# Seven gates of the attention branch given out ahead of the recurrences' merge, and that merge's first two outputs together

## The chip, the cores and the metric

One core of one Trainium2 chip runs the program. The metric is the device time of one execution in microseconds (us), the median over runs without a profile. The engines are TensorE (PE; its weight loads are PEld), VectorE (DVE), ScalarE (ACT), GpSimd (POOL) and SyncE (SP), which issues the loads.

## What is computed

Two transformer blocks run one after the other on 512 tokens of width 1024, in fp32. The change touches the second block, which has two layers (0 and 1). Cut to what matters here, a layer is:

```python
h = rmsnorm_2(x, norm_mix[l])
proj = h @ w_in[l]
aq, ak, av, iq, ik, iw, hq, hf, hi, hg, ga, gb = jnp.split(proj, split_points, axis=-1)
y_attn = dsa_attention(aq, ak, av, iq, ik, iw)          # top-k attention, 8 heads
...
o = hgrn2_chunked(q_h, k_in, v_h, log_f)                # gated recurrence, 4 heads
y_hgrn = (rmsnorm_2(o, hgrn_norm[l]) * silu(hg)).reshape(B, T, HGRN_WIDTH)
merged = sigmoid(ga) * (y_attn @ w_proj_attn[l]) + sigmoid(gb) * (y_hgrn @ w_proj_hgrn[l])
x = x + merged @ w_out[l]
h = rmsnorm_2(x, norm_ffn[l])
g, u = jnp.split(h @ w_ffn_in[l], 2, axis=-1)
x = x + (silu(g) * u) @ w_ffn_out[l]
```

A *gate* below is one 128-wide slice of ga or gb: eight gates for each of the two branches. The sigmoid is made from a tanh, and the factor of a half that is left is taken up at the residual sum.

## The kernel before, in words

Activations lie transposed, 128 features by 512 tokens to a tile. Every fp32 product is made from three matmuls: operands are split into a high part (a cast to fp32r) and a low part (what is left), and low x high, high x low and high x high are summed in PSUM.

**Weights** (`weights`, lines 133 to 154). A load of SP's queue brings 512 KB (or 256 KB for the output weights of a branch, which have four slices) into one of three `wraw` buffers. Per *set* of four 128x128 slices ScalarE casts the high part (line 149), and GpSimd or VectorE subtracts to give the low part (line 152). Which of the two is read off a rotation, `self.lows` (GpSimd, GpSimd, VectorE in the mixing stages), with a running count of sets. There are three buffers for the high and three for the low parts. A set feeds 12 matmuls of 128x512. All this is traced with high priority.

**Projections** (`project`, lines 184 to 196, the three matmuls on lines 193 to 195). Eight slices give 24 matmuls (a gate, from the two sets of one load), four slices give 12 (an output of a branch). The sum goes to one of four PSUM banks of the tag `mm`. `project_pair` (lines 198 to 217) makes two outputs at once and leaves the last slice of both to the end, so that the last input tile is wanted late.

**A gate** (`gate`, lines 694 to 698) is projected, evicted to SBUF by VectorE with the norm's factor (line 223) and put through tanh by ScalarE (line 697). Its tile is of the tag `g`, five slots.

**The merge of a branch** (`merge`, lines 700 to 718) makes `ahead` gates, then for each of eight outputs m the gate m + ahead, if there is one left, the projection of the branch, and the product (gate + 1) x projection on VectorE (line 710), with high priority. In the last merge of a layer the product is added to what the other branch left (line 715): on GpSimd for outputs 0 to 3, on VectorE for outputs 4 to 7, and from output 4 on all weight sets subtract on GpSimd. The sum is then split for the next projection: a cast on ScalarE (`mgh`, line 232), a subtraction on VectorE (`mgl`, line 233).

**A layer** (`second_mix`, lines 990 to 1016) traces, in this order: the attention (`dsa`, lane `a`, whose work tiles are of the tag `ua` with seven slots; its last tile is `aon`, line 969, and the next layer's first is `rows`, line 860, with four table products on lines 868 and 869), the four heads of the recurrence (lane `h`, tag `uh`, seven slots; a head's first tile is the `tanh` of its q, line 690, its last the `ry`, line 439), the recurrences' merge (two gates ahead) and the attention's merge (four gates ahead). After that comes the output projection (`residual`, lines 720 to 737), whose first two outputs are a pair.

**What sets the order.** A scheduler turns the traced program into one fixed queue per engine when the program is built: an instruction that was traced earlier has priority, one that is ready may run ahead of one that isn't. On the chip every queue is worked off in that order.

Of the kernel before, what the change touches and what calls it, by code (L numbers as in the profile page):

```python
# [21 lines left out]
KD = 8  # L22
# [48 lines left out]
class Builder:  # L71
# [340 lines left out]
    def recurrence(self, qi, kl, dec, v, AT, gate, gain, scale, name):  # L412
        nc = self.nc
        klT = self.u("rklT", shape=[P, NT, P])
        self.transpose4(kl, klT)
        kv = self.at([P, NT - 1, P])
        for t in range(NT - 1):
            nc.tensor.matmul(kv[:, t, :], klT[:, t, :], v[t], start=True, stop=True)
        S = self.u("rS", shape=[P, NT - 1, P])
        nc.vector.tensor_copy(S[:, 0, :], kv[:, 0, :])  # L420
        for t in range(1, NT - 1):
            nc.vector.scalar_tensor_tensor(S[:, t, :], S[:, t - 1, :], dec[:, t:t + 1], kv[:, t, :],
                                           op0=OP.mult, op1=OP.add)
        o = self.at([P, NT, P])
        for t in range(NT):
            nc.tensor.matmul(o[:, t, :], AT[:, t * P:(t + 1) * P], v[t], start=True, stop=t == 0)
            if t:
                nc.tensor.matmul(o[:, t, :], qi[:, t * P:(t + 1) * P], S[:, t - 1, :], start=False, stop=True)
        sq = self.u("rsq", shape=[P, NT, P])
        nc.scalar.activation(sq, o, AF.Square)  # L430
        ss = self.small("rss", NT)
        nc.vector.reduce_sum(ss, sq, axis=AX.X)
        nc.vector.tensor_scalar(ss, ss, scale / P, EPS, op0=OP.mult, op1=OP.add)
        r = self.rsqrt(ss, NT)
        on = self.u("ron", shape=[P, NT, P])
        nc.vector.tensor_tensor(on, o, r[:, :, None].to_broadcast([P, NT, P]), op=OP.mult)
        ps = self.transpose4(on.rearrange("p n c -> p (n c)"), None)
        y = self.u("ry")
        nc.vector.scalar_tensor_tensor(y, ps.rearrange("p n c -> p (n c)"), gain, gate, op0=OP.mult, op1=OP.mult)
        return self.split(y, name)  # L440

    def gla_head(self, B, q, k, v, gate, gain, name):
        nc = self.nc
        s = 1.0 / 16
# [44 lines left out]
    def hgrn_head(self, F, q, k, v, gate, gain, name):  # L489
# [6 lines left out]
        nc.vector.copy_predicated(AT, self.masks[:, T:2 * T], ps.rearrange("p n c -> p (n c)"))  # L496
        G = self.u("hG")
        for i, h in enumerate(LEVELS + (64,)):
            n = T // (2 * h)
            X = self.u("lvx")  # L500
            if h < 64:
                mk = self.masks[:, 2 * T + i * 256:2 * T + (i + 1) * 256].rearrange("p (n r) -> p n r", n=n)
            Fv, Gv, qv, kv, Xv, Av = [a.rearrange("p (n s r) -> p n s r", n=n, s=2) for a in (F, G, q, k, X, AT)]
            if h == 1:
# [30 lines left out]
        nc.vector.tensor_tensor(F, F, q, op=OP.mult)  # L535
        nc.gpsimd.tensor_tensor(G, G, k, op=OP.mult)
        return self.recurrence(F, G, dec, v, AT, gate, gain, 0.25, name)

# [152 lines left out]
        self.nc.vector.scalar_tensor_tensor(x, t, 1.0, x, op0=OP.add, op1=OP.mult)  # L691
        return x

    def gate(self, src, X):
        g = self.g("gate")
        self.evict(g, self.project(src, X))
        self.nc.scalar.activation(g, g, AF.Tanh, scale=0.5)
        return g

    def merge(self, W, X, WO, y, acc, ahead, last, alloc=None):  # L700
        nc = self.nc
        G = [self.gate(W[m], X) for m in range(ahead)]
        out = []
        for m in range(KD):
            if m + ahead < KD:
                G.append(self.gate(W[m + ahead], X))
            g = G[m] if acc else (alloc or self.t)("acc")
            ps = self.project(WO[m], y)
            with self.tc.high_priority():
                nc.vector.scalar_tensor_tensor(g, G[m], 1.0, ps, op0=OP.add, op1=OP.mult)  # L710
            if acc:
                eng = nc.vector if last and m + ahead >= KD else nc.gpsimd
                if last and m + ahead == KD:
                    self.lows = [nc.gpsimd]
                eng.tensor_tensor(acc[m], acc[m], g, op=OP.add)
                g = acc[m]
            out.append(self.split(g, "mg") if last else g)
        return out
# [271 lines left out]
    def second_mix(self, l, X):  # L990
        nc, A = self.nc, self.A
        W = A["w_in2"][l]
        it = iter(range(W.shape[0]))
        proj = lambda: self.project(W[next(it)], X)

        with self.on("a"):
            yattn = self.dsa(l, X)
        if self.pending:
            self.settle()
        hv = self.hv  # L1000
        yh = []
        for hd in range(4):
            F = self.scaled(proj(), "hf", self.i)
            k = self.i("hk")
            nc.scalar.activation(k, F, AF.Sigmoid, scale=-1.0)
            nc.scalar.activation(F, F, AF.Sigmoid)
            if l:
                nc.gpsimd.tensor_scalar(k, k, self.om[:, hd:hd + 1], None, op0=OP.mult)
                nc.vector.tensor_scalar(F, F, self.om[:, hd:hd + 1], self.lb[:, hd:hd + 1], op0=OP.mult, op1=OP.add)
            q = self.silu2(proj(), "hq")  # L1010
            v = [a[:, hd * P:(hd + 1) * P] for a in hv]
            g = self.silu2(proj(), "hg")
            yh.append(self.hgrn_head(F, q, k, v, g, self.half[:, 4 + l:5 + l], "yh"))

        acc = self.merge(A["w_gate2"][l, 1], X, A["w_po"][l, 1], yh, None, 2, False, self.i)
        return self.merge(A["w_gate2"][l, 0], X, A["w_po"][l, 0], yattn, acc, 4, True)

    def build(self, out):
        nc, A = self.nc, self.A
# [118 lines left out]
```

## Time and profile before

| | |
|---|---|
| median of the runs | 2522.63 us (2522.59 to 2522.65) |
| profiled execution | 2524.49 us |
| its span, first to last instruction | 2522.7 us |
| instructions | 31514 |
| PE, DVE, ACT, POOL busy | 2488.7, 1369.4, 1007.2, 614.2 us |
| granted TensorE clock, mean | 0.997 |

Times in the rows are counted from the start of the span. In layer 0 the attention and the recurrence take about 880 to 1178 us, the two merges 1178 to 1290, the output projection up to 1330; in layer 1 these are about 1700 to 2007, 2007 to 2118, and up to 2158. A row of the timeline has the start, the duration, the engine, the line of the kernel, the operation, what is written from what, the shapes, how many instructions are put together, and in brackets how long the engine was idle before it and what ended that. Matmuls overlap, so that their pace is read off their starts.

### The profile page before, as it was taken

The numbers are of one execution on the slowest core, as the hardware profiler recorded it, in microseconds if no ns is written. First come the engines' busy times: TensorE is split into PE (matmuls) and PEld (weight loads), VectorE is DVE, ScalarE is ACT, GpSimd is POOL, SyncE is SP. The second block draws the span as 40 slices with busy tenths as digits, with TensorE's granted clock in tenths as the row PEclk, the third lists the DMA queues.
The fourth block names the chain that finished last, engine by engine and source line by source line (L and its number), as shares of the span: only waits on it lengthen the run. The fifth ranks groups of instructions, "written<-read, shape, count | busy, mean of one in ns | idle before, by whom it ended". The sixth has DMA issues, their size and how long they took to land.

```text
span 2522.7 us, 31514 instructions
## 1 busy us (share of the span) xinstructions
PE 2488.7 (99%) x11742; PEld 2038.2 (81%) x11742; DVE 1369.4 (54%) x2696; ACT 1007.2 (40%) x1830; POOL 614.2 (24%) x548
## 2 busy tenths in 40 slices
PE   9999999999999999999999999999999999999999
PEld 7887888888888887777888888888777788888887
DVE  4675222477774558986244444334798624444432
ACT  5643333444443345543343333334554334333321
POOL 4004344511111102433361111010253435111100
PEclk9999999999999999999999999999999999999999
DMA  4112232322323322111332232332211133232333
GB/s 140 59 61 84 88 100 92 105 92 100 100 91 99 92 92 76 43 38 53 96 100 96 97 101 90 100 90 95 81 42 38 39 97 104 92 101 92 98 104 90
DMA packets 68298, 217.66 MB, mean 86 GB/s; under 512 B 7840, under 2 KB 8736, under 8 KB 68144
## 3 DMA queue, kind: packets, MB, share of 16 engines
q1 hardware_dynamic: 68144, 215.65, 26.7%
q8 instruction: 92, 1.51, 0.3%
q14 instruction: 62, 0.51, 0.1%
HBM read 213.52 MB, written 2.10 MB: 85 GB/s over the span
## 4 chain that ended last, share of the span: by engine, by line
PE 85%; DVE 7%; issue 3%; POOL 2%; ACT 2%; DMA 0%; SPq 0%; DVEq 0%; POOLq 0%; ACTq 0%
PE mm L195 23%; PE mm L194 23%; PE mm L193 23%; PE mm L168 3%; PE mm L169 3%; PE mm L170 3%; PE at L953 1%; DVE score L915 1%; PE at L965 1%; DVE m L914 1%; POOL wlo L152 1%; POOL hG L516 1%; PE at L260 1%; PE at L961 1%; DVE wlo L152 1%
## 5 line engine op out<-in xcount | busy, mean ns | idle before, releaser
L149 ACT CAST whi<-wraw 128x512 fp32r<-128x512 f32 (+3 forms) x824 | 502.1, 610 | 1120.6 <-PE mm L195 918.5
L194 PE MATMUL mm<-xl,whi 128*128 128x512 f32 x1920 | 758.2, 395 | 0.0
L193 PE MATMUL mm<-xh,wlo 128*128 128x512 f32 x1920 | 757.4, 395 | 0.0
L195 PE MATMUL mm<-xh,whi 128*128 128x512 f32 x1920 | 756.4, 394 | 0.0
L152 DVE TENSOR_TENSOR wlo<-wraw,whi 128x512 fp32r<-128x512 f32 (+2 forms) x597 | 428.3, 718 | 494.8 <-ACT whi L149 491.5
L152 POOL TENSOR_TENSOR wlo<-wraw,whi 128x512 fp32r<-128x512 f32 (+1 forms) x227 | 294.7, 1299 | 784.6 <-ACT whi L149 723.6
L194 PEld LDWEIGHTS mm<-xl,whi 128*128 128x128 f32 x1920 | 361.2, 188 | 73.8 <-issue 1.7
L195 PEld LDWEIGHTS mm<-xh,whi 128*128 128x128 f32 x1920 | 361.2, 188 | 73.7 <-issue 1.7
L193 PEld LDWEIGHTS mm<-xh,wlo 128*128 128x128 f32 x1920 | 361.1, 188 | 71.8 <-issue 0.7
L193 PE MATMUL mm<-acth,wlo 128*128 128x512 f32 x528 | 205.4, 389 | 0.0
L195 PE MATMUL mm<-acth,whi 128*128 128x512 f32 x528 | 205.4, 389 | 0.0
L194 PE MATMUL mm<-actl,whi 128*128 128x512 f32 x528 | 205.4, 389 | 0.0
L763 POOL TENSOR_TENSOR fg<-fg,rstd 128x512 f32<-128x512 f32 x44 | 56.6, 1287 | 425.9 <-ACT fg L762 425.9
L168 PE MATMUL mm<-wlo,xh 128*128 128x512 f32 (+2 forms) x384 | 144.1, 375 | 5.1 <-ACT lbe L813 3.6
L170 PE MATMUL mm<-whi,xh 128*128 128x512 f32 (+2 forms) x384 | 143.4, 374 | 0.0
L169 PE MATMUL mm<-whi,xl 128*128 128x512 f32 (+2 forms) x384 | 142.6, 371 | 0.0
L223 DVE TENSOR_TENSOR gate<-mm,rstd 128x512 f32<-128x512 f32 x56 | 38.7, 691 | 151.3 <-PE mm L195 150.5
L194 PEld LDWEIGHTS mm<-actl,whi 128*128 128x128 f32 x528 | 99.1, 188 | 20.7
L193 PEld LDWEIGHTS mm<-acth,wlo 128*128 128x128 f32 x528 | 99.1, 188 | 20.6
L195 PEld LDWEIGHTS mm<-acth,whi 128*128 128x128 f32 x528 | 99.1, 188 | 20.4
L298 POOL TENSOR_TENSOR acc<-acc,sq 128x512 f32<-128x512 f32 x39 | 57.6, 1478 | 200.5 <-ACT sq L295 199.6
L168 PEld LDWEIGHTS mm<-wlo,xh 128*128 128x128 f32 x384 | 72.8, 190 | 19.3 <-issue 4.5
(362 smaller groups left out, 3236.0 us busy)
## 6 DMA issues: line engine op xcount, KB each, us to landing
wraw<-in_w_ffn_in SPq DMA_DIRECT2D x88, 512.0 KB, 3.3
wraw<-in_w_gate SPq DMA_DIRECT2D x56, 512.0 KB, 3.3
wraw<-in_w_in SPq DMA_DIRECT2D x52, 512.0 KB, 3.2
wraw<-in_w_up SPq DMA_DIRECT2D x44, 512.0 KB, 3.2
wraw<-in_w_tok SPq DMA_DIRECT2D x32, 512.0 KB, 3.2
wraw<-in_w_ffn_out SPq DMA_DIRECT2D x32, 512.0 KB, 3.6
wraw<-in_w_down SPq DMA_DIRECT2D x16, 512.0 KB, 3.5
wraw<-in_w_po SPq DMA_DIRECT2D x32, 256.0 KB, 2.6
```

What stands on the lines that cost most here:

```text
L149: nc.scalar.copy(wh, raw[:, k:k + m, :])
L152: eng.tensor_tensor(wl, raw[:, k:k + m, :], wh.bitcast(F32), op=OP.subtract)
L168: nc.tensor.matmul(ps[t][:, 0:w], xh, wl, start=i == 0, stop=False)
L169: nc.tensor.matmul(ps[t][:, 0:w], xl, wh, start=False, stop=False)
L170: nc.tensor.matmul(ps[t][:, 0:w], xh, wh, start=False, stop=i == KD - 1)
L193: nc.tensor.matmul(ps, wl, xh, start=i == 0, stop=False)
L194: nc.tensor.matmul(ps, wh, xl, start=False, stop=False)
L195: nc.tensor.matmul(ps, wh, xh, start=False, stop=i == n - 1)
L223: self.nc.vector.tensor_tensor(out, ps, other, op=OP.mult)
L260: self.nc.tensor.transpose(ps[:, t, :], src[:, t * P:(t + 1) * P], self.ident)
L298: (nc.vector if d % 2 and len(acc) > 1 else nc.gpsimd).tensor_tensor(a, a, sq, op=OP.add)
L763: nc.gpsimd.tensor_tensor(g, g, self.rstd, op=OP.mult)
```

## The change

`merge` takes gates that were made before (`made`) and then makes only the rest; with `pair` its first two outputs are projected together. In each layer of the second block seven gates of the attention branch are traced ahead of the recurrences' merge, into tiles of the attention's tag `ua`; the attention's merge then has one gate left, which goes with output 0. The recurrences' merge is called with `pair`. The rule that gives the sums to VectorE from output 4 on is written with a constant and is the same as before for four gates ahead; it stays at output 4 for seven.

```diff
-    def gate(self, src, X):
-        g = self.g("gate")
+    def gate(self, src, X, alloc=None):
+        g = (alloc or self.g)("gate")
...
-    def merge(self, W, X, WO, y, acc, ahead, last, alloc=None):
-        nc = self.nc
-        G = [self.gate(W[m], X) for m in range(ahead)]
+    def merge(self, W, X, WO, y, acc, ahead, last, alloc=None, made=(), pair=False):
+        nc = self.nc
+        G = list(made) + [self.gate(W[m], X) for m in range(len(made), ahead)]
         out = []
+        pss = {}
         for m in range(KD):
             if m + ahead < KD:
                 G.append(self.gate(W[m + ahead], X))
             g = G[m] if acc else (alloc or self.t)("acc")
-            ps = self.project(WO[m], y)
+            if pair and m == 0:
+                pss.update(enumerate(self.project_pair([WO[0], WO[1]], y)))
+            ps = pss.pop(m) if m in pss else self.project(WO[m], y)
...
-                eng = nc.vector if last and m + ahead >= KD else nc.gpsimd
-                if last and m + ahead == KD:
+                eng = nc.vector if last and m >= KD // 2 else nc.gpsimd
+                if last and m == KD // 2:
                     self.lows = [nc.gpsimd]
...
-        acc = self.merge(A["w_gate2"][l, 1], X, A["w_po"][l, 1], yh, None, 2, False, self.i)
-        return self.merge(A["w_gate2"][l, 0], X, A["w_po"][l, 0], yattn, acc, 4, True)
+        with self.on("a"):
+            made = [self.gate(A["w_gate2"][l, 0, m], X, self.u) for m in range(self.SLOTS["a"])]
+        acc = self.merge(A["w_gate2"][l, 1], X, A["w_po"][l, 1], yh, None, 2, False, self.i, pair=True)
+        return self.merge(A["w_gate2"][l, 0], X, A["w_po"][l, 0], yattn, acc, len(made), True, made=made)
```

## Rows read from the trace of the kernel before

**Rows 1.** The page: busy time by engine; shares of the chain that ended last.

```profile
PE 2488.7 (99%) x11742; PEld 2038.2 (81%) x11742; DVE 1369.4 (54%) x2696; ACT 1007.2 (40%) x1830; POOL 614.2 (24%) x548
...
PE 85%; DVE 7%; issue 3%; POOL 2%; ACT 2%; DMA 0%; SPq 0%; DVEq 0%; POOLq 0%; ACTq 0%
```

**Rows 2.** Windows: length, busy PE PEld DVE ACT POOL, clock, DMA.

```profile
1110.00:1178.00 68.00, 64.26 (x405) 51.37 (x404) 54.82 (x130) 25.12 (x56) 32.49 (x36) 1.00 0.09 26
1178.00:1290.00 112.00, 112.00 (x494) 92.64 (x495) 36.61 (x53) 37.38 (x61) 41.89 (x33) 1.00 0.30 97
1936.00:2007.00 71.00, 67.46 (x400) 53.12 (x399) 50.80 (x123) 24.21 (x54) 32.90 (x36) 0.95 0.08 25
```

**Rows 3.** Timeline of PE, layer 0, fourth head: start, duration, instruction, idle before.

```profile
1156.82 0.39 PE L530 MATMUL at<-lvx 128*120 128x64 f32 x2 [0.85 <-DVE lvx L514]
...
1158.04 0.47 PE L193 MATMUL mm<-xh,wlo 128*128 128x512 f32 x1
```

**Rows 4.** Windows in layer 1, where the granted clock falls.

```profile
1940.00:1945.00 5.00, 3.28 (x23) 2.90 (x22) 4.04 (x8) 0.48 (x1) 4.69 (x6) 0.89 0.31 107
1945.00:1950.00 5.00, 5.00 (x17) 3.56 (x16) 2.02 (x6) 0.53 (x2) 2.46 (x5) 0.50 0.02 3
```

**Rows 5.** Timeline of DVE, layer 0, third and fourth head.

```profile
1100.02 0.69 DVE L223 TENSOR_TENSOR hq<-mm,rstd 128x512 f32<-128x512 f32 x1 [0.19 <-PE mm L195]
...
1126.76 0.69 DVE L223 TENSOR_TENSOR gate<-mm,rstd 128x512 f32<-128x512 f32 x1
...
1145.30 0.75 DVE L439 SCALAR_TENSOR_TENSOR ry<-at,half,hg 128x512 f32<-128x512 f32 x1 [0.26 <-PE at L260]
...
1166.93 0.69 DVE L969 TENSOR_TENSOR aon<-at,aden 128x512 f32<-128x512 f32 x1 [0.74 <-PE at L965]
...
1168.88 0.41 DVE L868 SCALAR_TENSOR_TENSOR tabC<-cos,rows 128x256 f32<-128x256 f32 x1
```

**Rows 6.** Timeline of ACT, the same stretch.

```profile
1145.40 0.63 ACT L690 ACTIVATE tanh<-hq 128x512 f32<-128x512 f32 x1
```

**Rows 7.** Groups of PE, 1110 to 1178: count, busy, mean ns, idle before.

```profile
L194 PE MATMUL mm<-xl,whi 128*128 128x512 f32 x30 | 12.7, 424 | 0.0
```

**Rows 8.** Timeline of SP's queue in the same stretch.

```profile
1149.96 0.33 SPq L861 DMA_DIRECT2D rows<-in_rows  x1
```

**Rows 9.** Timeline of PE, first output of the recurrences' merge, layer 0.

```profile
1177.87 0.50 PE L193 MATMUL mm<-yhh,wlo 128*128 128x512 f32 x1
```

**Rows 10.** Timeline of DVE, attention's merge, layer 0, outputs 3 to 5.

```profile
1275.27 0.69 DVE L710 SCALAR_TENSOR_TENSOR gate<-gate,mm 128x512 f32<-128x512 f32 x1 [2.03 <-PE mm L195]
1279.28 0.69 DVE L233 TENSOR_TENSOR mgl<-acc,mgh 128x512 fp32r<-128x512 f32 x1 [3.33 <-ACT mgh L232]
1279.89 0.68 DVE L710 SCALAR_TENSOR_TENSOR gate<-gate,mm 128x512 f32<-128x512 f32 x1
1280.61 1.08 DVE L715 TENSOR_TENSOR acc<-acc,gate 128x512 f32<-128x512 f32 x1
...
1282.98 0.68 DVE L710 SCALAR_TENSOR_TENSOR gate<-gate,mm 128x512 f32<-128x512 f32 x1
```

**Rows 11.** Timeline of POOL, the same outputs.

```profile
1276.06 1.29 POOL L152 TENSOR_TENSOR wlo<-wraw,whi 128x512 fp32r<-128x512 f32 x1 [1.43 <-issue]
1277.31 1.29 POOL L715 TENSOR_TENSOR acc<-acc,gate 128x512 f32<-128x512 f32 x1
1279.85 1.29 POOL L152 TENSOR_TENSOR wlo<-wraw,whi 128x512 fp32r<-128x512 f32 x1 [1.25 <-ACT whi L149]
```

**Rows 12.** Timeline of ACT, the same outputs.

```profile
1278.63 0.62 ACT L232 CAST mgh<-acc 128x512 fp32r<-128x512 f32 x1 [2.70 <-POOL acc L715]
1279.15 0.62 ACT L149 CAST whi<-wraw 128x512 fp32r<-128x512 f32 x1
```

**Rows 13.** Timeline of PE, first pair of the output projection, layer 0.

```profile
1293.20 0.39 PE L209 MATMUL mm<-mgh,whi 128*128 128x512 f32 x1
1293.67 0.50 PE L207 MATMUL mm<-mgh,wlo 128*128 128x512 f32 x1
```

## The prediction

> **What bounds the kernel now.** I read the page's busy times and its chain first: TensorE is busy for 2488.7 of 2522.7 us and carries 85% of the chain that ended last [rows 1]. Its work stays the same here, so only its waits can move. The windows by stage say where these are. In the stretch from the merge of the recurrences to the end of the attention's merge TensorE is busy for all of 112 us, with 494 matmuls, 0.227 us each; in the two stretches in which the last recurrence head and the last attention block run, it stands idle for 68.00 - 64.26 = 3.7 us (layer 0) and 71.00 - 67.46 = 3.5 us (layer 1) [rows 2]. The timeline of TensorE shows the kind of these waits: at 1156.82 a small matmul of the recurrence waits 0.85 us for VectorE, and the gate's matmul of 1158.04 stands behind it in the queue [rows 3]. The order is fixed when the program is built, and a matmul that could fill the gap sits behind the one that waits. Between 1945 and 1950 the granted clock is 0.50, the lower level of 1.2 GHz, after TensorE was idle for 1.7 of the 5 us ahead of it [rows 4]. At half speed for 5 us, some 2.5 us are lost.
>
> **Part 1: seven gates go ahead.** Per layer 7 x 24 = 168 matmuls, 14 weight sets (cast on ScalarE, subtraction on GpSimd or VectorE), 7 loads of 512 KB on SP's queue, 7 evictions and 7 tanh move ahead of the recurrences' merge: past its 8 gates and 8 outputs, on every queue. Nothing is added. A set feeds 12 matmuls whichever gate it belongs to, so SP's queue and the casts keep their rate, and the move of the loads costs nothing by itself. The gain would be filler for the waits. But filler was not lacking: in before the gates of the recurrences' merge already stand in this place, the first is evicted at 1126.76 [rows 5], and the gap of 1156 had a gate's matmul right behind it [rows 3]. Another gate in that place is the same filler. I take 0; the best case is that all idle time goes, -3.7 and -3.5 us [rows 2], and the half clock with it, -2.5 us [rows 4].
>
> The new tiles are not free as early. The tanh of a head's q waits for its tile: q is evicted at 1100.02, yet its tanh runs at 1145.40, right after the last tile (ry) of the previous head came at 1145.30 [rows 5, 6], although tanh needs nothing else. So tiles of one tag are given out in the program's order. The gates' tiles then come after the attention's last one, aon, at 1166.93 [rows 5]; until then up to four products stay in PSUM's four mm banks, 96 matmuls. Before used some 90 of such filler between 1110 and 1178 (this line's 30 and two more lines of 30 [rows 7]), and a few more of the merge's, so the banks just suffice: 0, and up to +1 us per layer if they don't. Two evictions of 0.69 us leave the stretch before 1166 and fall behind it: 0, bounds -1.4 and +1.4 us per layer on VectorE; TensorE has gates to do meanwhile. The load of the next layer's rope rows, the next tile of this tag, went out at 1149.96 [rows 8]; it now waits behind the gates for a freed tile, in the attention's merge. Its four table products (0.41 us each, the first at 1168.88 [rows 5]) go there too: 0, bounds -1.7 and +1.7 us, once. SP's later loads stand behind that wait; with three load buffers they run ahead of it, so 0.
>
> **Part 2: the first two outputs together.** Before, the last part of output 0 is mixed with a gate's matmuls, and two matmuls at such a change take 0.1 us longer: the one at 1177.87 has 0.50 us [rows 9], where its like have 0.39 [rows 13]. Now ten gates stand ahead of the pair, 240 matmuls, of which some 90 are done when the last head is; the pair starts 150 x 0.227 = 34 us later, the mixing goes, and with it twice 0.1: -0.2 us per layer. The pairing itself then hides nothing.
>
> **Part 3: the attention's merge loses its gates.** This is the term that decides. Before, outputs 0 to 3 each have a gate beside them: 36 matmuls, 8.17 us. The chain from an output's product (line 710) over the sum on GpSimd, the cast and the low half (line 233) takes 1275.27 to 1279.28 plus 0.61 until the next product can start at 1279.89: 4.62 us [rows 10]. It fits into 8.17, not into the 12 x 0.227 = 2.72 us of an output alone. And VectorE takes low half and next product in that order: at 1279.89 the product of output 4, whose matmuls were done about 1278.0, comes right behind the low half of output 3 [rows 10]. After the change outputs 1 to 3 stand as output 4 does now. Each transition is then a loop of queues that each wait for the other:
> - 0 to 1, with GpSimd's weight subtraction ahead of the sum (1276.06, then 1277.31 [rows 11]): 4.62 us.
> - 1 to 2: the rotation (GpSimd, GpSimd, VectorE; the count before output 4 stays as it is) gives this subtraction to VectorE, so the sum starts at once: 0.72 to the sum, 1.32 to the cast, 0.65 to the low half, 0.61 to the next product [rows 10 to 12], 3.30 us.
> - 2 to 3 and 3 to 4: the cast of a weight set stands behind the cast of the output: 0.52, then 0.70 to the subtraction, 1.25 to the sum, 1.32 to the next cast [rows 11, 12], 3.79 us each.
> Sum 15.5 us; before it was 3 x 2.72 + 4.62 = 12.78 of the same work (gates apart). The lag grows by 2.7 us. From output 4 on, the loop runs at 1279.89 to 1282.98 = 3.09 us against 2.72 [rows 10], as before, and there all reserve of weights is used up: the last set of the output projection's pair already comes late, TensorE goes from 1293.20 to 1293.67 where 0.23 is due, a wait of 0.24 us [rows 13]. So what is added shows in full: **+2.7 us per layer**. Bounds: 0, if VectorE takes the next product first and the loop opens; 4 x 4.62 - 12.78 = +5.7, if each transition takes as long as the first.
>
> **Sum.** 2 x (2.7 - 0.2) = +5.0 us. On the profiled execution (2524.49 us, a span of 2522.7 with 1.8 around it) that is 2529.5; the median of the runs without a profile is 1.86 below, so 2522.63 + 5.0 = **2527.6 us**. Measurement tells 0.2% (5.05 us) from no change, so this is just no change, with slower close by.
>
> **Rivals.**
> - *The loop opens.* VectorE takes the next product while the low half waits; TensorE stays full. For it: the gates are out of the way, and GpSimd's load (a sum of 1.29 and two thirds of a subtraction of 1.29 [rows 11], 2.2 us of 2.72) fits. Against: the order at 1279 [rows 10]. It gives 2522.6 - 0.4 = 2522.2.
> - *The waits in the recurrences go*, since evictions and tables leave that stretch, and the clock doesn't fall: half of 7.3 us of idle time and 2.5 us of clock, with the loop open: 2522.2 - 3.7 - 2.5 = 2516. For it: VectorE is busy for 54.8 of 68 us there [rows 2]; against: the order is fixed as before.
> - *GpSimd and VectorE stop each other* (slower). The sum on VectorE at 1280.61 takes 1.08 us while GpSimd subtracts from 1279.85 to 1281.14; the low half with two inputs of the same size takes 0.69 beside an idle GpSimd [rows 10, 11]. In outputs 0 to 3 GpSimd will be busy most of the time, so low halves and subtractions on VectorE get this 0.4 us at least, in each of four transitions: 2 x 4 x 0.4 = 3.2, 2530.8; with a whole GpSimd instruction of 1.29 each, 2538. It decides once GpSimd runs through without a gap. The Trainium skill ("SBUF — State Buffer", section "SBUF: two separate sides") says that whichever of a GpSimd instruction and a VectorE instruction with two SBUF inputs starts first holds the shared port pair and the other is fully blocked; the trace agrees with it at 1280.61, where the sum ends 0.55 us after the subtraction, and the higher end is what that page would make of it.
>
> **How the numbers follow.** The loop as worked out 0.58 (its own range is 2523.5 to 2531.5, and half of it lies beyond 2527.7); the loop open 0.20; fewer waits in the recurrences 0.12; GpSimd and VectorE in each other's way 0.10. Faster by over 0.2%: 0.12, the third case; slower: 0.36, half of the first and two thirds of the fourth; within: 0.52, the rest. The range leaves out the low end of the third and the high end of the fourth: 2516.5 to 2532.5.
>
> **What would show it.** Products of outputs 1 to 4 at line 710 that start right behind a low half of line 233, 3.3 to 4.6 us apart, and waits of TensorE for a subtraction (line 152) in the last outputs and the pair of the output projection, 2 to 3 us per layer: right. Products 2.72 us apart and no wait: the loop is open. Gates' evictions only after aon: the tile order is right. Idle time from the last head's projections to its end well off 3.7 and 3.5 us: part 1 is wrong.

## The result, and the profile after

The changed kernel takes 2536.2 us (median of four runs, 2533.4 to 2536.6) against 2522.6 us of the kernel before on the same chip: a ratio of 1.0051 (95% interval 1.0039 to 1.0063), 13.6 us slower. The forecast was 2527.6 us with a range up to 2532.5: slower had been given the second largest chance (0.36), and the time lies outside the range. The profiled execution took 2536.1 us, with a span of 2534.3.

The page of the kernel after, busy time by engine (before: [rows 1]), and its windows, with the columns of [rows 2]:

```profile
PE 2493.1 (98%) x11742; PEld 2041.0 (81%) x11742; DVE 1375.5 (54%) x2696; ACT 1007.3 (40%) x1830; POOL 614.0 (24%) x548
```

```profile
1110.00:1178.00 68.00, 62.36 (x395) 50.33 (x394) 53.38 (x124) 24.09 (x54) 32.46 (x36) 1.00 0.09 29
...
1280.00:1302.00 22.00, 20.08 (x82) 14.63 (x82) 12.12 (x16) 7.41 (x14) 10.21 (x8) 1.00 0.34 109
1936.00:2007.00 71.00, 66.24 (x389) 53.40 (x389) 50.84 (x115) 23.72 (x53) 30.06 (x35) 0.90 0.09 30
```

The same window behind the attention's merge, in the kernel before:

```profile
1280.00:1302.00 22.00, 21.92 (x97) 17.81 (x97) 14.22 (x16) 9.12 (x16) 11.68 (x10) 1.00 0.35 120
```

The instructions are the same (11742 matmuls). Two kinds of stretch have become worse, in each layer: the last head of the recurrences, with 5.6 us idle in place of 3.7 (layer 0) and 4.8 in place of 3.5 (layer 1), and the end of the attention's merge, where 15 matmuls fewer fit into 22 us.

Busy time alone hides two losses, matmuls at half clock and such as start late without a recorded wait. So the table below uses **lost time**: for each TensorE instruction the time from its start to the start of the next, less the median of this for its kind (line, shape) in the same run, added up over a stretch. It is worked out from the whole trace of each profiled run.

```
                     heads 1-3     last head     both    end of attention's
                     L0     L1     L0     L1     merges  merge, L0   L1    time - before   ratio (95%)
before               11.7   12.4   6.7    11.0   -0.3    1.1   1.1         0
after                11.7   12.5   8.6    14.7   -0.3    4.4   4.2     +13.6   1.0051 (1.0039-1.0063)
e1_four_ahead        11.7   12.5   8.6    14.9   -0.3    1.1   1.1      +5.4   1.0019 (1.0010-1.0028)
e2_gates_between     11.7   12.5   7.7    10.4    0.1    4.1   4.2      +7.6   1.0028 (1.0017-1.0039)
e3_pair_alone        11.6   12.5   8.2    12.0   -0.2    1.1   1.1      +2.4   1.0009 (1.0000-1.0018)
e4_sums_vector       11.7   12.5   9.7    14.7   -0.3    1.6   1.0      +5.6   1.0020 (1.0011-1.0029)
e5_plain_evict       11.8   12.5   9.5    12.8   -0.3    4.4   4.3     +12.2   1.0047 (1.0034-1.0059)
e6_early_tiles       11.7   12.5   7.9    11.4   -0.3    1.1   1.1      +0.6   1.0001 (0.9992-1.0010)
e7_late_tiles        11.7   12.5   8.2    14.7   -0.3    1.4   1.1      +3.9   1.0014 (1.0005-1.0022)
e8_no_pair           11.7   12.5   9.9    12.5   -0.3    4.3   4.1     +10.7   1.0040 (1.0027-1.0052)
e9_no_subtraction    11.7   12.5   8.3    12.8   -0.3    4.4   4.2     +11.7   1.0044 (1.0031-1.0056)
e10_low_vector        8.6    7.1   8.0    12.2   17.5    1.1   1.1     +12.0   1.0049 (1.0035-1.0063)
e11_both              8.8    8.0   9.5    13.9    0.4    1.1   1.1      -4.3   0.9985 (0.9976-0.9994)
e12_heads_only        8.5    7.7   7.7    14.6    3.0    1.1   1.1      -1.9   0.9995 (0.9986-1.0004)
```

Stretches: 990-1110 and 1800-1925; 1110-1180 and 1925-2015; 1180-1280 and 2015-2110 together; 1280-1345 and 2110-2180. Times are differences of medians against the kernel before, run beside each (2521.8 to 2523.2 us). What is left out of the columns differs by up to 2 us from before, mostly ahead of 990, where the code is the same and the granted clock is 0.50 for 6.8 us in some profiles and for 3.4 in others. Each run has its own medians: in e10, e11 and e12 the attention's matmuls of 128x512 (`at<-kT,qT`) have 0.43 us in place of before's 0.48, and with before's medians the four heads' columns of these three rows, added up, are 1.7 to 2.8 us lower (last heads 7.2 and 11.3, 8.6 and 13.0, 7.1 and 14.0); e7's last heads become 7.8 and 14.3.

After against before: 3.4 + 3.1 us at the end of the attention's merge, 1.9 + 3.7 us in the last head, 12.1 in all (added up before rounding); the span grew by 11.6.

**The end of the merge.** Timeline of VectorE in the kernel after, layer 0, outputs 0 to 5 (start, duration, instruction, idle before; line 713 is the product that was 710, 718 the sum that was 715; compare [rows 10]):

```profile
1268.46 0.69 DVE L713 SCALAR_TENSOR_TENSOR gate<-gate,mm 128x512 f32<-128x512 f32 x1 [2.03 <-PE mm L195]
1272.42 0.69 DVE L233 TENSOR_TENSOR mgl<-acc,mgh 128x512 fp32r<-128x512 f32 x1 [3.28 <-ACT mgh L232]
1273.03 0.68 DVE L713 SCALAR_TENSOR_TENSOR gate<-gate,mm 128x512 f32<-128x512 f32 x1
...
1276.15 0.69 DVE L233 TENSOR_TENSOR mgl<-acc,mgh 128x512 fp32r<-128x512 f32 x1
1276.76 0.68 DVE L713 SCALAR_TENSOR_TENSOR gate<-gate,mm 128x512 f32<-128x512 f32 x1
...
1280.18 0.69 DVE L233 TENSOR_TENSOR mgl<-acc,mgh 128x512 fp32r<-128x512 f32 x1 [0.41 <-ACT mgh L232]
1280.79 0.68 DVE L713 SCALAR_TENSOR_TENSOR gate<-gate,mm 128x512 f32<-128x512 f32 x1
1284.03 0.69 DVE L233 TENSOR_TENSOR mgl<-acc,mgh 128x512 fp32r<-128x512 f32 x1 [2.56 <-ACT mgh L232]
1284.64 0.68 DVE L713 SCALAR_TENSOR_TENSOR gate<-gate,mm 128x512 f32<-128x512 f32 x1
```

Each product starts right behind the low half of the output before it: the loop of queues. The transitions, from one product to the next, are 4.57, 3.73, 4.03 and 3.85 us, 16.2 in all. The sum of the second transition, on GpSimd, takes 1.67 us in place of 1.29 (timeline of GpSimd):

```profile
1273.79 1.67 POOL L718 TENSOR_TENSOR acc<-acc,gate 128x512 f32<-128x512 f32 x1 [2.06 <-DVE gate L713]
```

TensorE runs out of weight sets behind it (timeline of PE; [rows 13] has 0.47 us from the first of such a pair to the second, here it is 1.1):

```profile
1285.93 0.50 PE L193 MATMUL mm<-yah,wlo 128*128 128x512 f32 x1 [0.76 <-POOL wlo L152]
...
1298.39 0.50 PE L207 MATMUL mm<-mgh,wlo 128*128 128x512 f32 x1 [0.75 <-POOL wlo L152]
```

**The last head.** A head's result is brought to its norm: VectorE makes an rsqrt in eleven small steps on 128x4 elements (lines 433 and 250 to 254), multiplies (`ron`, line 436), and TensorE transposes `ron` (line 260). VectorE in the kernel after, layer 0 (compare [rows 5]), with GpSimd's and TensorE's rows of the same moment:

```profile
1167.12 0.69 DVE L972 TENSOR_TENSOR aon<-at,aden 128x512 f32<-128x512 f32 x1 [2.06 <-PE at L968]
1167.72 1.28 DVE L223 TENSOR_TENSOR gate<-mm,rstd 128x512 f32<-128x512 f32 x2
...
1174.24 0.16 DVE L252 TENSOR_TENSOR rsq_w<-rss,rsq_y 128x4 f32<-128x4 f32 x1
...
1174.84 1.21 DVE L252 TENSOR_TENSOR rsq_w<-rss,rsq_y 128x4 f32<-128x4 f32 x1
...
1176.55 0.69 DVE L436 TENSOR_TENSOR ron<-at,rsq_y 128x512 f32<-128x512 f32 x1
```

```profile
1174.74 1.29 POOL L152 TENSOR_TENSOR wlo<-wraw,whi 128x512 fp32r<-128x512 f32 x1 [11.75 <-ACT whi L149]
```

```profile
1177.30 0.66 PE L260 MATMUL at<-csts,ron 128*128 128x128 f32 x4 [1.25 <-DVE ron L436]
```

The first gate is evicted right behind `aon`, not 40 us ahead of it as in [rows 5]. And a step of the head's rsqrt on 128x4 elements, 0.16 us as its like at 1174.24, takes 1.21 us while GpSimd subtracts; it ends with that subtraction, `ron` is late by 1.05 us, and TensorE waits 1.25. In layer 1 the step takes 0.98 and the wait 0.73. Before, GpSimd's subtraction came behind the last step, which ended at 1174.94:

```profile
1176.62 1.30 POOL L152 TENSOR_TENSOR wlo<-wraw,whi 128x512 fp32r<-128x512 f32 x1 [11.51 <-ACT whi L149]
```

**Layer 1 and its clock.** A head works through several levels; in each VectorE and GpSimd fill a tile `lvx` and GpSimd carries on a product `hG`, for small matmuls of TensorE (line 530). GpSimd, VectorE and TensorE in the last head's first levels, then two windows of the kernel after:

```profile
1979.52 1.29 POOL L152 TENSOR_TENSOR wlo<-wraw,whi 128x512 fp32r<-128x512 f32 x1 [9.00 <-ACT whi L149]
1980.77 0.92 POOL L507 TENSOR_TENSOR lvx<-lvx,hk 128x256 f32<-128x256 f32 x1
```

```profile
1979.74 1.34 DVE L518 TENSOR_TENSOR hf<-hf 128x256 f32<-128x256 f32 x1
...
1983.86 0.43 DVE L518 TENSOR_TENSOR hf<-hf 128x256 f32<-128x256 f32 x1 [1.89 <-POOL hG L516]
```

```profile
1986.55 0.62 PE L530 MATMUL at<-lvx 128*124 128x64 f32 x4 [1.98 <-POOL lvx L515]
```

```profile
1985.00:1990.00 5.00, 3.45 (x23) 3.42 (x23) 4.79 (x11) 1.40 (x3) 3.91 (x6) 0.80 0.00 0
1990.00:1995.00 5.00, 5.00 (x19) 3.92 (x19) 2.63 (x7) 0.81 (x2) 2.38 (x4) 0.52 0.00 0
```

A weight subtraction now stands in GpSimd's queue right ahead of the head's first level. VectorE's step at 1979.74 takes 1.34 us beside that subtraction, its like at 1983.86 0.43. The level starts at 1980.77, 1.1 us after its input from VectorE was there, and TensorE waits 1.98 us in the levels. In the kernel before the longest wait in this head's levels is 1.06 us:

```profile
1988.83 0.69 PE L530 MATMUL at<-lvx 128*96 128x64 f32 x6 [1.06 <-DVE AT L532]
```

Behind the wait of 1.98 us the granted clock goes to 0.50, the level of 1.2 GHz, from 1988 to 1994.8. Before had one such stretch in this layer ([rows 4], 1944 to 1951); the kernel after has that one (1947 to 1954) and this one. The four timed runs show the same: three at a mean clock of 0.996 with 2536.1 to 2536.6 us, one at 0.998 with 2533.4.

### The profile page after: what moved, and what is told of

Read it like the earlier page. It is cut to its first block, busy times and chain, and to the rows that moved or that the text cites. A ratio compares the mean times of both kernels' runs of the same rounds, so it can differ in the third digit from the quotient of the medians.

```text
span 2534.3 us, 31505 instructions
## 1 busy us (share of the span) xinstructions
PE 2493.1 (98%) x11742; PEld 2041.0 (81%) x11742; DVE 1375.5 (54%) x2696; ACT 1007.3 (40%) x1830; POOL 614.0 (24%) x548
```

## The experiments

Three theories: **A**, the merge's loop (some 6.5 us); **B**, the gates' late tiles (free only behind `aon`), which change the order of the work in the last head; **C**, GpSimd's subtraction beside the rsqrt. Rivals are that one of them is all of it, or that the move of the gates ahead is the cause, whatever their tiles.

### Taking the loop away, or doing it alone

e1: four gates ahead in place of seven.

```diff
-made = [... for m in range(self.SLOTS["a"])]
+made = [... for m in range(4)]
```

> The changed kernel with four gates of the attention ahead in place of seven; the other four again stand beside outputs 0 to 3 of the attention's merge. Split theory (merge loop about 6.5 us of the 13.6, the rest in the recurrences' end and in the half clock): the loop is gone and the rest stays, 2536.2 - 6.5 = about 2529.7 us, with transitions between the products of outputs 0 to 3 back at about 8 us and no TensorE waits over 0.2 us behind 1280. Rival 'all of it is the merge loop' (the waits in the recurrences would have moved, not grown): 2522.6 us. Rival 'all of it is the recurrences' end': about 2536 us.

Measured 2528.3 us, +5.4. The end of the merge loses 1.1 us again, with 21.92 of 22 us busy; the last head is as in the kernel after.

```profile
1280.00:1302.00 22.00, 21.92 (x98) 17.81 (x97) 13.99 (x17) 9.83 (x18) 10.89 (x9) 1.00 0.36 117
```

e2: the seven gates between the two merges, no pair.

```diff
+acc = self.merge(..., yh, None, 2, False, self.i)
 with self.on("a"):
     made = [...]
-acc = self.merge(..., yh, None, 2, False, self.i, pair=True)
```

> The seven gates stand between the two merges in place of ahead of the first, in the same tiles, and the first two outputs do not go together: the recurrences' end is that of the kernel before, the attention's merge still has only one gate beside its outputs. Split theory: 2522.6 + 6.5 = about 2529.1 us, lost TensorE time in the merge's last part about 4.4 and 4.2 us as in the changed kernel (1.1 before). Rival 'all is the loop': 2536 us. Rival 'all is the recurrences' end': 2522.6 us.

Measured 2530.4 us, +7.6, with the loop there (4.1 and 4.2 us; the window below is shifted by 2 us) and a last head near that of before: 1.0 more in layer 0, 0.6 less in layer 1.

```profile
1278.00:1300.00 22.00, 20.10 (x83) 14.66 (x82) 12.09 (x16) 7.42 (x14) 10.20 (x8) 1.00 0.33 109
```

e4: all sums of the attention's merge on VectorE, the weight subtractions on GpSimd.

```diff
-eng = nc.vector if last and m >= KD // 2 else nc.gpsimd
-if last and m == KD // 2:
+n = 0 if made else KD // 2
+eng = nc.vector if last and m >= n else nc.gpsimd
+if last and m == n:
```

> The changed kernel, with the sums of all outputs of the attention's merge in both layers on VectorE and the weight subtractions on GpSimd from output 0 on, as they were from output 4 on only. Loop theory (the transitions of 3.7 to 4.6 us are GpSimd's sum behind its weight subtraction): transitions of about 3.1 us from output 0 on, 4 x 3.1 = 12.4 in place of 16.2 per layer, so 2536.2 - 2 x 3.8 = about 2528.6 us. Rival 'GpSimd and VectorE stop each other' (the shift of work does not help, sums and low halves on VectorE are prolonged beside the subtraction of GpSimd): transitions stay above 3.6 us and the time at 2534 us or more.

Measured 2528.4 us, +5.6. The products of layer 0 start at 1268.63, 1271.66, 1275.51, 1278.93 and 1282.03 (timeline of VectorE, three of them below): 3.03, 3.85, 3.42 and 3.10 us, 13.4 for four transitions in place of 16.2. In the second the sum, now on VectorE, takes 1.56 us beside a subtraction of GpSimd, and rope tables follow it; the expected 12.4 was a little short, but the loss is nearly gone (1.6 and 1.0 us, 1.1 before).

```profile
1275.51 0.68 DVE L713 SCALAR_TENSOR_TENSOR gate<-gate,mm 128x512 f32<-128x512 f32 x1
...
1278.93 0.68 DVE L713 SCALAR_TENSOR_TENSOR gate<-gate,mm 128x512 f32<-128x512 f32 x1
...
1282.03 0.68 DVE L713 SCALAR_TENSOR_TENSOR gate<-gate,mm 128x512 f32<-128x512 f32 x1
```

So A holds and is about half of the result: taken away in two ways it gives back 8 us (6.5 and 6.0 of it in the merge's columns), done alone (e2) it costs 7.6.

### The pair

e3: the kernel before with `pair=True` on the recurrences' merge. e8: the changed kernel without it.

> The kernel before with the pair alone: outputs 0 and 1 of the recurrences' merge go together, the gates as they were. My step for the pair (twice 0.1 us per layer from the mixing, nothing hidden): 2522.2 us, no difference that can be measured. Rival 'with only two gates ahead the pair has nine more matmuls (2.0 us) that do not need the last head, and these fill waits': up to 2 us per layer, 2518.6 us.

> The changed kernel without the pair. With seven gates and then two more ahead of it the pair comes some 34 us after the last head's output, so it hides nothing: within 0.5 us of the changed kernel, 2536.2 us. Rival 'the pair costs a wait for weight sets as it does alone' (1.53 us per layer there): 2533 us.

e3: 2525.3 us, +2.4. Both theories fall. The pair, close behind two gates, holds two weight sets up to its last matmuls, where one output holds one. ScalarE casts the next three sets only then, GpSimd subtracts two of them one behind the other, and TensorE waits 1.37 us at the gate behind the pair, 1.36 in layer 1 (timelines of ScalarE, GpSimd and TensorE):

```profile
1179.45 1.66 ACT L149 CAST whi<-wraw 128x512 fp32r<-128x512 f32 x3 [1.55 <-PE mm L209]
```

```profile
1180.14 2.96 POOL L152 TENSOR_TENSOR wlo<-wraw,whi 128x512 fp32r<-128x512 f32 x2 [14.95 <-ACT whi L149]
```

```profile
1181.47 0.50 PE L193 MATMUL mm<-xh,wlo 128*128 128x512 f32 x1 [1.37 <-POOL wlo L152]
```

e8: 2533.9 us, +10.7 for +13.6: the time of the rival, not of the theory. But the rival's wait isn't there: the merges, the only place where the pair stands, lose -0.3 us with it and without it, and TensorE's longer waits in the last heads are the same in both (1.5 and 1.25 us in layer 0; 1.36, 1.16, 1.98 and 0.73 in layer 1, each within 0.02). What differs is the granted clock. The kernel after has two half-clock stretches of 6.8 us in layer 1; e8 has one there, and one of 3.4 us in layer 0. Whether leaving the pair out moves the clock, or another run of the same kernel would, one profile doesn't tell, so the 2.9 us stay open.

### Tiles, or the move?

e6: four gates of the attention ahead in the gates' own tiles, which are free early; the recurrences' merge takes the attention's tiles. e7: the kernel before with only that last part.

```diff
 e6
-with self.on("a"):
-    made = [self.gate(..., self.u) for m in range(self.SLOTS["a"])]
-acc = self.merge(..., yh, None, 2, False, self.i, pair=True)
+made = [self.gate(...) for m in range(4)]
+with self.on("a"):
+    acc = self.merge(..., yh, None, 2, False, self.i, pair=True, galloc=self.u)
 e7
+with self.on("a"):
+    acc = self.merge(..., yh, None, 2, False, self.i, galloc=self.u)
```

> The changed kernel with four gates of the attention ahead, in the gates' own tiles, which are free early; the recurrences' merge takes the attention's freed tiles for its gates instead. Pair as in the changed kernel. Theory 'late tiles': the gates ahead are evicted during the heads as before, lost TensorE time in the recurrences' end is as before (6.7 and 11.0 us), no loop in the merge, so about 2522.4 us. Rival 'it is the move of the gates ahead, whatever their tiles': the recurrences' end stays at 8.6 and 14.7 us and the time at that of the run with four gates ahead, 2528.3 us.

> The kernel before with one edit: the eight gates of the recurrences' merge stand in the attention's freed tiles; order, counts and pair as before. Theory 'late tiles alone do it': evictions only behind aon, lost time in the recurrences' end 8.6 and 14.7 us as in the changed kernel, about 2528 us. Rival 'it needs the move': 2522.6 us, with the recurrences' end at 6.7 and 11.0 us.

e6: 2523.7 us, +0.6, no difference. Evictions of gates on VectorE stand where [rows 5] has them:

```profile
1126.21 0.69 DVE L223 TENSOR_TENSOR gate<-mm,rstd 128x512 f32<-128x512 f32 x1
...
1143.81 0.69 DVE L223 TENSOR_TENSOR gate<-mm,rstd 128x512 f32<-128x512 f32 x1
1166.40 0.69 DVE L972 TENSOR_TENSOR aon<-at,aden 128x512 f32<-128x512 f32 x1 [0.74 <-PE at L968]
```

e7: 2527.1 us, +3.9, with nothing moved and no pair. The first evictions come behind aon, GpSimd's subtraction stands ahead of the last head of layer 1, and TensorE waits the same 1.98 us (e7's VectorE, GpSimd, TensorE):

```profile
1165.94 0.69 DVE L972 TENSOR_TENSOR aon<-at,aden 128x512 f32<-128x512 f32 x1 [2.06 <-PE at L968]
1166.55 1.28 DVE L223 TENSOR_TENSOR gate<-mm,rstd 128x512 f32<-128x512 f32 x2
```

```profile
1973.20 1.29 POOL L152 TENSOR_TENSOR wlo<-wraw,whi 128x512 fp32r<-128x512 f32 x1 [9.01 <-ACT whi L149]
1974.45 0.91 POOL L507 TENSOR_TENSOR lvx<-lvx,hk 128x256 f32<-128x256 f32 x1
```

```profile
1980.21 1.47 PE L530 MATMUL at<-lvx 128*124 128x64 f32 x6 [1.98 <-POOL lvx L515]
```

So B holds: the waits of 1.98 us for `lvx` (layer 1) and of 1.5 us for `hG` (layer 0) are in every run whose gates in the heads have late tiles (after, e1, e4, e5, e7, e8, e9) and in none of before, e2, e3, e6, where the waits at the like places are 1.06 to 1.07 and 0.92 to 0.93 us.

### The wait for ron

e5: the seven gates' evictions at ordinary priority. e9: gate 4's two low halves as copies on ScalarE; the kernel then leaves out these two subtractions in each layer.

```diff
 e5, in gate(), where alloc is given
-self.evict(g, self.project(src, X))
+self.nc.vector.tensor_tensor(g, ps, self.rstd, op=OP.mult)
 e9, in weights(), while gate 4 is made
-eng.tensor_tensor(wl, raw[:, k:k + m, :], wh.bitcast(F32), op=OP.subtract)
+nc.scalar.copy(wl, raw[:, k:k + m, :])
```

> The changed kernel, with the seven gates' evictions at ordinary priority, so that VectorE's order no longer puts three of them between aon and the last head's ron. In the changed kernel TensorE waits 1.25 and 0.73 us for ron there. If the bundle of evictions behind aon is what makes the recurrences' end longer: these two waits go and the time falls by about 2 us against the changed kernel (2536.2), lost time from 1110 to 1180 back from 8.6 to about 7. Rival 'the changed order of the weight sets is the cause' (the low half on GpSimd ahead of the head's level, the 1.98 us wait at 1984): within 1 us of 2536.2, or worse because gates now hold PSUM banks longer.

> The changed kernel, but the low halves of gate 4's two weight sets (512 columns each, on GpSimd in layer 0, at 1174.74 and 1179.42) are plain copies on ScalarE: the subtraction of these two sets per layer is left out, all else stays. In the changed kernel a step of the last head's rsqrt on VectorE, 0.16 us as its like, takes 1.21 us at 1174.84 (0.98 in layer 1) while GpSimd subtracts gate 4's first set. Theory 'GpSimd holds VectorE up there': all steps of this rsqrt take 0.16 to 0.2 us again, ron comes 1.05 and 0.8 us earlier, TensorE's wait for ron falls from 1.25 to about 0.2 us (0.73 to about 0), the time by about 1.9 us against the changed kernel, to 2534. Rival 'ron is late because the evictions stand ahead of the rsqrt': the wait stays above 0.8 us.

e5: 2535.4 us, +12.2 for +13.6. The waits for ron stay at 0.95 and 0.92 us, and a step of the rsqrt still takes 1.17 us beside GpSimd (1176.52): my first reading, a bundle of evictions ahead of ron, falls.

e9: 2533.4 us, +11.7 for +13.6, as C expects. VectorE's steps and TensorE's transpose of ron (line numbers are 4 higher):

```profile
1175.11 0.16 DVE L256 TENSOR_TENSOR rsq_w<-rss,rsq_y 128x4 f32<-128x4 f32 x1
1175.31 0.16 DVE L257 SCALAR_TENSOR_TENSOR rsq_w<-rsq_w,rsq_y 128x4 f32<-128x4 f32 x1
1175.50 0.16 DVE L258 SCALAR_TENSOR_TENSOR rsq_y<-rsq_w,rsq_y 128x4 f32<-128x4 f32 x1
1175.70 0.69 DVE L440 TENSOR_TENSOR ron<-at,rsq_y 128x512 f32<-128x512 f32 x1
```

```profile
1176.44 0.66 PE L264 MATMUL at<-csts,ron 128*128 128x128 f32 x4
```

All steps take 0.16 us and the wait for ron is gone in both layers. The time fell by 1.9 us against the kernel after, as expected; the two waits were 1.25 + 0.73 us. The half-clock stretches lie otherwise in this profile (3.4 us in layer 0, 3.4 and 6.8 in layer 1), but add up to the same 13.6 us in these heads.

This wait is not the tiles' doing: e6, with early tiles, has it too (1.23 us), and e7, with late tiles and no gates ahead, has none. It comes with gates ahead. Before, matmuls of the recurrences' own output stood between two gates' sets, and GpSimd's subtraction ran at 1176.62, behind the rsqrt; with only gates in the queue it runs 1.9 us earlier, onto it.

Taken singly, the loop costs some 6.5 us, the late tiles 3.9 (e7) and the wait for ron 1.9 (e9): 12.3 of the 13.6. With the clock's stretches differing from run to run, that they are just additive isn't shown.

### A version that beats both

If GpSimd's subtractions are what holds the heads up, their low halves belong on VectorE. e10: so from the heads to the end of their merge. e12: in the heads alone. e11: e6 with this, in the heads and the four gates ahead. So `mixing()` stands behind the recurrences' merge in e10, ahead of it in e11 and e12.

```diff
 yh = []
+self.feeding()
 ...
+self.mixing()
```

> The kernel before with one edit: the low halves of all weight sets from the recurrence heads to the end of their merge go on VectorE (0.69 us each) and none on GpSimd (1.29 us, during which VectorE's instructions take longer). If GpSimd's subtractions hold the heads up (they stand in GpSimd's queue ahead of the heads' levels and prolong VectorE's): idle TensorE time in the recurrences' end falls from 6.7 and 11.0 us by 1 to 2 us per layer, about 2519.5 us, faster than both kernels. Rival 'VectorE is what the heads wait for' (busy 54.8 of 68 us there): five more low halves of 0.69 us make it later, 2525 us.

> The kernel before with the low halves of the heads' weight sets alone on VectorE; gates and merge as before, none ahead. Theory 'filler is lacking': the gain of 3.0 and 5.3 us in the first two thirds and a loss of 8 to 10 us per layer behind the last head, as in the run with the merge's sets on VectorE too: about 2532 us. Rival 'the loss there came from the merge's own low halves on VectorE': 2522.6 - 8.3 + 2.5 = 2517 us.

> Four attention gates ahead in the gates' own tiles and the pair, as in the run with early tiles; and the low halves of the weight sets of the recurrence heads and of these four gates on VectorE, as in the run before (there from the heads to the end of the merge). In that run the heads' first two thirds lost 3.0 and 5.3 us less (990 to 1110, 1800 to 1925), but then the matmuls that don't need the last head ran out: 9.6 and 7.9 us were lost right behind it. Theory 'filler is lacking there, and gates ahead are filler': 96 matmuls more, 22 us, cover these 17.5 us, and about 2523.7 - 8.3 + 2 = 2517.5 us remain, faster than both kernels. Rival 'VectorE's low halves make the last heads late whatever stands beside them': 2525 us or more.

e10: 2533.7 us, +12.0. The first three heads lose 3.0 and 5.3 us less; the windows of heads 1 to 3 show TensorE at 116.98 of 120 and 122.57 of 125 us (before: 114.59 and 118.93). Behind the last head TensorE then waits for `ron`, for `yhh` and for a subtraction that is now VectorE's:

```profile
1188.86 1.12 PE L260 MATMUL at<-csts,ron 128*128 128x128 f32 x4 [2.82 <-DVE ron L436]
...
1191.47 1.65 PE L193 MATMUL mm<-yhh,wlo 128*128 128x512 f32 x3 [1.49 <-ACT yhh L232]
1197.03 0.50 PE L193 MATMUL mm<-xh,wlo 128*128 128x512 f32 x1 [1.38 <-DVE wlo L152]
```

e12: 2521.2 us, -1.9, between its two expectations, and its interval takes in no change: the gain of the first three heads stays, but the last heads lose 0.4 and 3.0 us more than before (by before's medians), and the loss in the merges is 3.0 us and not 17.5. So most of e10's loss did come from the merge's own sets on VectorE, and some from the missing filler.

e11: **2518.7 us, 0.9985 (0.9976 to 0.9994)**, faster than both kernels, near the 2517.5 expected. With four gates ahead (and e6's tiles and pair, which alone changed nothing) the merges lose 0.4 us, not e12's 3.0; the last heads still lose 1.9 and 2.0 us more than before (by before's medians). Between e12 and e11 lie 2.4 us, with runs that overlap (2518.1 to 2523.8 and 2517.6 to 2520.4). Windows of e10 and of e11 behind the last head:

```profile
1180.00:1200.00 20.00, 13.76 (x59) 10.33 (x58) 10.80 (x27) 4.69 (x8) 0.00 (x0) 0.83 0.12 43
```

```profile
1180.00:1200.00 20.00, 20.00 (x98) 16.74 (x98) 9.39 (x24) 6.34 (x11) 5.16 (x4) 0.97 0.27 82
```

## Why the prediction was wrong, point by point

- **Part 3, the loop: right, a little small.** Its place, its order and the two engines that carry it are as said. The forecast was 15.5 us for four transitions and +2.7 us per layer; measured were 16.2 (layer 0) and 16.0 (layer 1), and +3.4 and +3.1. The step that was short is the transition from 1 to 2, given as 3.30 us "so the sum starts at once": it takes 3.73. GpSimd's sum does start at once (1273.79), but VectorE has just begun the weight subtraction that the rotation gives it (1273.63), and the sum takes 1.67 us where its like take 1.29. e2 and e4 bear the term out. In the forecast the loop was +5.4 of 5.0 us; it is some 6.5 of 13.6.
- **Part 1, the gates ahead: this step failed.** Right were that filler was not lacking (31 full matmuls a line in the window of the last head for 30 before [rows 7], and no gain) and that the tiles come only behind aon. Wrong was the price of the late tiles, "0, bounds -1.4 and +1.4 us per layer", and that gates ahead had no other. I priced the two evictions that move, 0.69 us each on VectorE. But the order of all queues is made with the tiles: with a tile that comes late, gates' products fall elsewhere in TensorE's order, and their weight sets elsewhere in GpSimd's. Late tiles alone (e7) cost 3.9 us, and their waits of 1.5 and 1.98 us are those of the kernel after. The gates ahead as such add the wait for ron, 1.25 and 0.73 us (e9: 1.9 us). In the place of 0 the last head lost 1.9 and 3.7 us.
- **The half clock was counted as a gain only.** I had -2.5 us if it went [rows 4]; that a new wait could bring a second stretch had no term. In the kernel after it did, 6.8 us at 1.2 GHz. Since other waits hide in such a stretch, its net price is not read off directly; the run at 0.998 is 2.7 to 3.2 us faster than those at 0.996.
- **The rival "GpSimd and VectorE stop each other": right mechanism, mostly wrong place.** I put it in the merge, on low halves, at 0.4 to 1.29 us. There the low halves kept their 0.69 us, and a sum of GpSimd lost 0.38 us to a weight subtraction on VectorE. It struck a step of 0.16 us in the rsqrt of the last head, which took 1.21 (0.98), at a total of 1.25 + 0.73 us of waits (e9). The Trainium skill ("SBUF — State Buffer", section "SBUF: two separate sides") says that of a GpSimd instruction that reads SBUF and a VectorE one with two SBUF inputs the second is fully blocked until the first ends; the trace agrees: the subtraction runs from 1174.74 to 1176.03, the step, begun at 1174.84, ends at 1176.05.
- **Part 2, the pair: right in its place, -0.2 us not seen.** In the changed kernel it ends at 1216 without a wait, and the merges lose as much without it; why the time without it was 2.9 us lower is open (e8). Alone it would have cost 2.4 us (e3), which I had not thought of.
- **The moved load and the rope tables: as said, 0.** The tables fell into the merge (two of the four beside GpSimd's sums, at 1.5 us in place of 0.41), but layer 1, which has none, has the same loop within 0.2 us.
- **The range** reached to 2532.5. The loop at the upper bound that part 3 gives, +5.7 us per layer, makes 2533.6 by itself, so its "own range" up to 2531.5 did not follow from its bounds. And it took the uncertain terms of part 1 as small and of both signs, where the runs showed two causes, late tiles and a GpSimd subtraction on the rsqrt, of the same sign.

What stays open: what decides whether the clock falls behind the wait of 1.98 us (e5 and e8 have the wait and no second stretch in layer 1), why e8 is 2.9 us faster, and how the 5 us of e7's last heads divide between the clock and the waits. Its layer 1 has 13.6 us at half clock where before has 6.8, so an estimate of the clock's part is at most half the difference, 3.4 us. Not tried: seven gates ahead in tiles that are free early, for which the kernel has no seven such tiles.

## What to carry to other kernels

Before moving work ahead as filler, look for the waits that it would fill: if matmuls already stand behind them, the order is the limit and more filler gives nothing; here gates ahead paid only when another edit had used the filler up (e12 to e11, 2.4 us, with e6's tiles and pair along with them). The work that is moved may have been the cover of a loop where it stood: sum up one round of the queues there, and compare it with the matmuls that remain. And ask of a new buffer not only how large it is but when it comes free, since a late one reorders every queue.

## What was not expected of the hardware

- A VectorE step on 128x4 elements took over 7 times as long, 1.21 us for 0.16, when it met a GpSimd subtraction of 1.29 us. The chain of eleven such steps was met in after, e1, e4, e5, e6 and e8, and in before missed by 1.7 us.
- The same holds the other way by less: GpSimd's sum took 1.67 us for 1.29 when VectorE's subtraction began 0.17 us ahead of it (2108.26 and 2108.09, layer 1).
- Behind waits of TensorE of 1.5 and 2.0 us the granted clock was 0.50 for 3 to 10 us (e7: 1980 to 1990), and in other runs behind the same waits it stayed at 1.00 (layer 0 of after and e1, layer 1 of e5 and e8).
- Taking 18 us of GpSimd's 48.7 busy us out of heads 1 to 3 (30.7 in e10) gave TensorE 2.4 us there, in layer 1 3.6, though VectorE got the work.
